# Keeping x in two of five raw weight buffers, and another order of the seven products

## The chip, the core and the metric

The kernel runs on one core of one Trainium2 chip. The metric is the device time of one execution in microseconds (us), the median of the runs shown. The engines are named as in the profile: PE (TensorE) multiplies, PEld is its weight load, DVE (VectorE) and ACT (ScalarE) work element by element, POOL (GpSimd) computes and issues DMAs, SP (SyncE) issues DMAs.

## What is computed

One layer of a streaming encoder over 256 tokens of width 2048, in float32. Cut to what matters here, with `F = 5632`:

```python
def swiglu(h, w_gate, w_up, w_down):
    return (jax.nn.silu(h @ w_gate) * (h @ w_up)) @ w_down

x = x + 0.5 * swiglu(rms_norm(x, ffn1_norm), ffn1_w_gate, ffn1_w_up, ffn1_w_down)
h = rms_norm(x, mix_norm);  proj = h @ w_in            # 2048 -> 4096: u, q, k, v
y_ssm = s5_mixer(u, ...);   y_sb = stick_breaking_attention(q, k, v)
x = x + concat(rms_norm(y_ssm), rms_norm(y_sb)) @ w_out
x = x + 0.5 * swiglu(rms_norm(x, ffn2_norm), ffn2_w_gate, ffn2_w_up, ffn2_w_down)
x = x + rms_norm((p @ w_ple_proj) * sigmoid(rms_norm(x, ple_norm) @ w_ple_gate))
```

## The kernel before

**Split products.** Every weight block comes from DRAM as float32 into a `raw` buffer (128 partitions, four 128-row tiles of 512 columns, 1 MB). A block is split in two halves of two tiles: ACT casts the half to `whi` (L168), DVE takes the rest `wlo = raw - whi` (L171). A half meets both token tiles (`t` = 0, 1) in 12 matmuls of 128x512: hi by hi (L292), hi by lo (L293), lo by hi (L297). There are four `whi` and four `wlo` buffers, so ACT and DVE can be four halves ahead of PE and no more.

**Stages.** `ffn(1)` runs eleven column blocks `f` of gate and up, while `s5_prep` makes the mixer's constants beside it, then four column blocks `n` of down. Then come the mixer, `ffn(2)` of the same shape, and the last gate (`ple`). The transposed hidden rows `hT` are put together by small DMAs from `mid` (L216), into which DVE transposes (L203).

**The seven products.** In `ffn(2)`, for `f` from 1 on, `gemm_seven` treats the first chunk of 512 rows of gate and up together: with the blocks b11, b21 (gate) and b12, b22 (up), seven products P1 to P7 stand for eight. Each is six matmuls (L452, L453, L455). Their weights are either half a raw block (`whi`, `wlo`), or sums of halves: t1 = b11 + b12, t2 = t1 + b22, t4 = t2 + b21, t3 = b12 + b22 (DVE, L459, two `sum` buffers), which are split into `shi` and `slo` (three buffers each). The left sides are the activations or four sums of them that `sum_forms` makes once. The other three chunks of gate and up go the plain way. P1, P2, P4 and P5 gather in `acc` banks, P6, P7, P3 and P8 in two double `aux` banks. At the end of a block DVE adds the `aux` bank into `hh` (L545), multiplies (L547) and transposes (L203).

**Memory.** `raw` has three buffers (8 KB a partition each). x stays in eight tiles of its own, `xt[t][n]` (16 KB a partition in all), from its load (`load_x`, L144) to the end.

**Order.** The code is written in program order, with generators (`put_off`, `step`) that place small work between halves. A scheduler then fixes the order on each engine and gives out the buffers when a program is built; at run time each engine works through its list in order and waits on semaphores.

Of the kernel before, what the change touches and what calls it, by code (L numbers as in the profile page):

```python
# [16 lines left out]
P = 128  # L17
# [9 lines left out]
NB = 512  # L27
# [6 lines left out]
def layer_kernel(ctx: ExitStack, tc: tile.TileContext, a: dict, shapes: dict, out: bass.AP):  # L34
# [18 lines left out]
    xpool = ctx.enter_context(tc.tile_pool(name="xres", bufs=1))  # L53
# [183 lines left out]
    def first_quarters(w, xn):  # L237

        rest = com("h")
        raws = [wp.tile([P, 4, NB], F32, tag="raw", name=uid("raw"), bufs=3) for _ in range(2)]  # L240
# [36 lines left out]

    def weight_halves(w, k0, nk, n0, own=None):

        raw = wp.tile([P, 4, NB], F32, tag="raw", name=uid("raw"), bufs=3)  # L280
        src = w[k0 * P : (k0 + nk) * P, n0 : n0 + NB].rearrange("(j p) n -> p j n", p=P)
        nc.sync.dma_start(raw[:, :nk, :], src)
        return weight_split(raw, nk, own)
# [122 lines left out]
        def rs(self, t):  # L406
            return self.r[:, t : t + 1]

    def sum_forms(parts):

        hi, lo = parts
        whole, sums = com("h"), com("h")
        u = whole.rearrange("p (j t m) -> p j t m", j=4, t=TT)
        nc.vector.tensor_tensor(
            out=whole.rearrange("p (j t) -> p j t", j=4), in0=hi.bitcast(F32), in1=lo.bitcast(F32), op=ALU.add
        )
        s = sums.rearrange("p (z j m) -> p z j m", z=4, j=2)
        up, down = u[:, :2], u[:, 2:]
        for z, (x, y, op) in enumerate((
            (up[:, :, 1], down[:, :, 1], ALU.subtract), (s[:, 0], up[:, :, 0], ALU.subtract),  # L420
            (up[:, :, 0], up[:, :, 1], ALU.subtract), (down[:, :, 0], s[:, 1], ALU.add),
        )):
            nc.vector.tensor_tensor(out=s[:, z], in0=x, in1=y, op=op)
        both = halves("n")
        split(*both, sums.rearrange("p (z t) -> p z t", z=4))
        return both

    def gemm_seven(act, sums, ws, n0, nkt, pool, first, second):

        raws = []  # L430
        for w in ws:
            raw = wp.tile([P, 4, NB], F32, tag="raw", name=uid("raw"), bufs=3)
            nc.sync.dma_start(raw, w[: 4 * P, n0 : n0 + NB].rearrange("(j p) n -> p j n", p=P))
            raws.append(raw)
        b11, b21, b12, b22 = (raw[:, 2 * h : 2 * h + 2, :] for raw in raws for h in range(2))
        parts = act(0)

        def whole(k, t):
            return [[u[:, 2 * k + j, t * P : (t + 1) * P] for j in range(2)] for u in parts]

        def summed(z):
            return [[u[:, z, j * P : (j + 1) * P] for j in range(2)] for u in sums]

        def product(ps, left, src, own, stop):
            hi, lo = (
                (pool if own else wp).tile([P, 2, NB], F32R, tag=s, name=uid(s), bufs=3 if own else None)
                for s in (("shi", "slo") if own else ("whi", "wlo"))
            )
            split(hi, lo, src)
            lh, ll = left  # L450
            for j in range(2):
                nc.tensor.matmul(ps, lhsT=lh[j], rhs=hi[:, j], start=j == 0, stop=False)  # L452
                nc.tensor.matmul(ps, lhsT=ll[j], rhs=hi[:, j], start=False, stop=False)  # L453
            for j in range(2):
                nc.tensor.matmul(ps, lhsT=lh[j], rhs=lo[:, j], start=False, stop=stop and j == 1)  # L455

        def add(x, y):
            t = pool.tile([P, 2, NB], F32, tag="sum", name=uid("sum"), bufs=2)
            nc.vector.tensor_tensor(out=t, in0=x, in1=y, op=ALU.add)  # L459
# [21 lines left out]
        step()  # L481
        put_off(0, first, p1, p67)
        for w, banks, fresh in ((ws[0], [p2, p4], False), (ws[1], [p38[:, :NB], p38[:, NB:]], True)):
            for k0 in range(4, nkt, 4):
                part = act(k0 // 4)
                for half in list(weight_halves(w, k0, 4, n0)):
                    begin = k0 == 4 and half[0] == 0
                    end = k0 + 4 >= nkt and half[0] == 1
                    for t in range(TT):
                        gemm_half({t: banks[t]}, (part, half), (t,), fresh and t == 1 and begin, end)  # L490
                    step()
            if not fresh:
                put_off(0, second, p2, p4, p5)
        return p38

    def ffn(i, xn, nxt, bg=None):
        wg, wu, wd = (a[f"ffn{i}_w_{s}"][0] for s in ("gate", "up", "down"))
# [22 lines left out]
        for f in range(NF):  # L520
# [5 lines left out]
            if sevens and f:  # L526
                sg, hh = com("sg"), com("h")
                gate_cols, up_cols = ([u[:, t * NB : (t + 1) * NB] for t in range(TT)] for u in (sg, hh))

                def opened(p1, p67, g=gate_cols, u=up_cols):  # L530
                    nc.scalar.copy(g[0], p1)
                    nc.vector.tensor_tensor(out=u[0], in0=p67[:, :NB], in1=g[0], op=ALU.add)
                    nc.vector.tensor_tensor(out=u[1], in0=p67[:, NB:], in1=u[0], op=ALU.add)

                def gated(p2, p4, p5, g=gate_cols, u=up_cols, hh=hh):
                    for z, (ps, other) in enumerate(((p2, g[0]), (p4, u[1]))):
# [3 lines left out]
                    nc.vector.tensor_tensor(  # L540
                        out=v, in0=p5.unsqueeze(1).to_broadcast([P, TT, NB]), in1=v, op=ALU.subtract
                    )

                p38 = gemm_seven(xn, sums, (wg, wu), f * NB, KD, sevens, opened, gated)
                nc.vector.tensor_tensor(out=hh, in0=p38, in1=hh, op=ALU.add)  # L545
                for t in range(TT):
                    nc.vector.scalar_tensor_tensor(  # L547
                        out=up_cols[t], in0=up_cols[t], scalar=xn.rs(t), in1=gate_cols[t], op0=ALU.mult, op1=ALU.mult
# [12 lines left out]
            if f == 0 and not bg:  # L561
                both = gemm_pair(xn, ((wg, 0), (wu, 0)), KD)
                pg = next(both)
                sums = sum_forms(xn(0))
            else:
                pg = gemm_block(xn, wg, f * NB, KD, first)
            sg = com("sg")
# [15 lines left out]
                )  # L583
            put_off(2, turned, hp, f, hh)

        def act(k):
            hi, lo = halves("h")
            split(in_32(hi), in_32(lo), hT[k // 2][:, k % 2 * 4 : k % 2 * 4 + 4])
            return hi, lo

        for n in range(ND):
# [743 lines left out]
    for n, side in ((0, 0), (1, 0), (0, 1), (1, 1), (2, 0), (2, 1), (3, 0), (3, 1)):  # L1335
        y, r = ((yss, rss), (ysb, rsb))[side]
        ps = next(both) if n < 2 and not side else gemm_block(lambda k: y[k], sides[side], n * NB, SW // P)
        for t in range(TT):
            nc.vector.scalar_tensor_tensor(
                out=xt[t][n], in0=ps[t], scalar=r[0][:, t : t + 1], in1=xt[t][n], op0=ALU.mult, op1=ALU.add  # L1340
            )
        if side:
            put_off(0 if n == ND - 1 else 2, n2.block, n)
    atp.close()
    mix.close()
# [205 lines left out]
```

## Time and profile before

| | us |
|---|---|
| median of 3 runs | 1872.24 (1870.79 to 1873.25) |
| the profiled execution | 1872.24, its span 1870.4 |
| PE busy | 1859.4 (99%), 9134 matmuls by the page |
| DVE busy | 1310.4 (70%) |
| ACT busy | 996.5 (53%) |
| POOL busy | 50.4 (3%) |
| DMA moved | 400.06 MB, mean 214 GB/s |

The span runs from the first to the last instruction; 1.8 us of the profiled execution's time lie outside it. PE is busy almost all of the span, so a time that falls or rises must show as a gap, or a slower pace, in PE's row of matmuls. The other engines' busy shares say how much room they have to be early.

### The profile page before, as it was taken

The page shows a single profiled execution, that of the slowest core. Times are in us where ns is not written, and L with a number is a line of the kernel's source. Part 1 is how long each engine was busy: PE and PEld are TensorE (multiplying, and loading weights), DVE is VectorE, ACT ScalarE, POOL GpSimd, SP SyncE. Part 2 cuts the span into 40 slices and gives each one's busy share as a digit, 9 for nine tenths or more (in the row PEclk, how much of TensorE's full clock was granted, in tenths as well). Part 3 has the DMA queues.
Part 4 walks back from the last instruction along what each step waited for, and adds up shares of the span by engine and source line. Part 5 has one row for each costly group of instructions (what it writes and reads, how often), then busy time and mean ns, then how long its engine had stood idle before and what let it go on. Part 6 is the DMA issues. An engine that isn't in the chain of part 4 may idle for free.

```text
span 1870.4 us, 23938 instructions
## 1 busy us (share of the span) xinstructions
PE 1859.4 (99%) x9134; PEld 1536.3 (82%) x9134; DVE 1310.4 (70%) x1527; ACT 996.5 (53%) x1151; POOL 50.4 (3%) x84
## 2 busy tenths in 40 slices
PE   9999999999999999999999999999999999999998
PEld 7888888888888888878888888888888888888887
DVE  8867665455576776687567678778787866777655
ACT  7444444444456665456695555445454555666554
POOL 0011000000000000010020000000000000000000
PEclk9999999999999999999999999999999999999999
DMA  8788867766655666675645666575666675656563
GB/s 323 242 278 268 267 208 222 231 217 200 217 196 199 212 199 244 185 248 163 222 147 189 218 205 221 203 220 186 203 205 208 225 228 203 204 202 212 189 224 124
DMA packets 230387, 400.06 MB, mean 214 GB/s; under 512 B 26401, under 2 KB 50337, under 8 KB 229985
## 3 DMA queue, kind: packets, MB, share of 16 engines
q1 hardware_dynamic: 227824, 392.81, 63.7%
q0 software_dynamic: 1728, 4.33, 0.7%
q8 instruction: 71, 1.16, 0.3%
q10 hardware_dynamic: 720, 1.41, 0.2%
q14 instruction: 44, 0.35, 0.1%
HBM read 369.26 MB, written 9.83 MB: 203 GB/s over the span
## 4 chain that ended last, share of the span: by engine, by line
PE 92%; ACT 3%; DVE 2%; DMA 1%; SPq 1%; issue 1%; POOL 0%; DVEq 0%; ACTq 0%; POOLq 0%
PE acc L292 26%; PE acc L297 26%; PE acc L293 26%; PE aux L293 3%; PE aux L292 3%; PE aux L297 3%; ACT whi L168 1%; SPq L1061 1%; PE acc L455 1%; DMA raw<-in_w_in 1%; PE aux L452 1%; PE acc L452 1%; PE acc L453 1%; PE aux L455 1%; PE aux L453 1%
## 5 line engine op out<-in xcount | busy, mean ns | idle before, releaser
L171 DVE TENSOR_TENSOR wlo<-raw,whi 128x1024 fp32r<-128x1024 f32 x656 | 798.2, 1224 | 458.9 <-ACT whi L168 455.3
L168 ACT CAST whi<-raw 128x1024 fp32r<-128x1024 f32 x656 | 686.2, 1053 | 758.7 <-PE acc L293 607.9
L292 PE MATMUL acc<-whi,nhi 128*128 128x512 f32 x1408 | 551.0, 391 | 1.2 <-ACT whi L260 0.5
L293 PE MATMUL acc<-whi,nlo 128*128 128x512 f32 x1408 | 548.2, 389 | 0.0
L297 PE MATMUL acc<-wlo,nhi 128*128 128x512 f32 x1408 | 384.4, 389 | 0.0
L292 PE MATMUL acc<-whi,hhi 128*128 128x512 f32 x816 | 317.6, 389 | 0.0
L293 PE MATMUL acc<-whi,hlo 128*128 128x512 f32 x816 | 317.5, 389 | 0.0
L292 PEld LDWEIGHTS acc<-whi,nhi 128*128 128x128 f32 x1408 | 264.3, 188 | 58.3 <-ACT whi L168 1.7
L297 PEld LDWEIGHTS acc<-wlo,nhi 128*128 128x128 f32 x1408 | 264.2, 188 | 55.6 <-DVE wlo L171 0.4
L293 PEld LDWEIGHTS acc<-whi,nlo 128*128 128x128 f32 x1408 | 264.4, 188 | 54.0
L297 PE MATMUL acc<-wlo,hhi 128*128 128x512 f32 x816 | 221.0, 389 | 0.0
L297 PEld LDWEIGHTS acc<-wlo,hhi 128*128 128x128 f32 x816 | 152.8, 188 | 32.5 <-DVE wlo L171 0.9
L293 PEld LDWEIGHTS acc<-whi,hlo 128*128 128x128 f32 x816 | 153.2, 188 | 32.0
L292 PEld LDWEIGHTS acc<-whi,hhi 128*128 128x128 f32 x816 | 153.1, 188 | 31.8
L171 DVE TENSOR_TENSOR hlo<-hT,hhi 128x1024 fp32r<-128x1024 f32 x88 | 107.1, 1218 | 0.0
L168 ACT CAST hhi<-hT 128x1024 fp32r<-128x1024 f32 x88 | 91.8, 1044 | 0.5 <-PE acc L455 0.4
L292 PE MATMUL aux<-whi,nhi 128*128 128x512 f32 x160 | 62.2, 389 | 0.0
L293 PE MATMUL aux<-whi,nlo 128*128 128x512 f32 x160 | 62.2, 389 | 0.0
L297 PE MATMUL aux<-wlo,nhi 128*128 128x512 f32 x160 | 49.3, 389 | 0.0
L171 DVE TENSOR_TENSOR slo<-sum,shi 128x1024 fp32r<-128x1024 f32 x40 | 48.6, 1214 | 0.4 <-ACT shi L168 0.2
L168 ACT CAST shi<-sum 128x1024 fp32r<-128x1024 f32 x40 | 42.1, 1052 | 11.5 <-DVE sum L459 11.4
L297 PEld LDWEIGHTS aux<-wlo,nhi 128*128 128x128 f32 x160 | 30.0, 188 | 6.2
(312 smaller groups left out, 1314.5 us busy)
## 6 DMA issues: line engine op xcount, KB each, us to landing
raw<-in_ffn_w_up SPq DMA_DIRECT2D x88, 1024.0 KB, 5.9
raw<-in_ffn_w_down SPq DMA_DIRECT2D x88, 1024.0 KB, 5.0
raw<-in_ffn_w_gate SPq DMA_DIRECT2D x86, 1024.0 KB, 5.4
raw<-in_w_in SPq DMA_DIRECT2D x32, 1024.0 KB, 5.5
raw<-in_w_out SPq DMA_DIRECT2D x16, 1024.0 KB, 5.1
raw<-in_w_ple_gate SPq DMA_DIRECT2D x16, 1024.0 KB, 5.1
hT<-mid SPq DMA_DIRECT2D x160, 64.0 KB, 5.0
h<-mid SPq DMA_DIRECT2D x176, 32.0 KB, 3.4
```

Source lines behind the costliest of these rows:

```text
L168: copy = nc.scalar.copy(hi, src)
L171: nc.vector.tensor_tensor(out=lo, in0=src, in1=hi.bitcast(F32), op=ALU.subtract)
L292: nc.tensor.matmul(ps[t], lhsT=lh, rhs=hi[:, j, cols], start=start and j == 0, stop=False)
L293: nc.tensor.matmul(ps[t], lhsT=ll, rhs=hi[:, j, cols], start=False, stop=False)
L297: nc.tensor.matmul(ps[t], lhsT=lh, rhs=lo[:, j, cols], start=False, stop=stop and j == 1)
L452: nc.tensor.matmul(ps, lhsT=lh[j], rhs=hi[:, j], start=j == 0, stop=False)
L453: nc.tensor.matmul(ps, lhsT=ll[j], rhs=hi[:, j], start=False, stop=False)
L455: nc.tensor.matmul(ps, lhsT=lh[j], rhs=lo[:, j], start=False, stop=stop and j == 1)
L1061: nc.sync.dma_start(zt[0][p1 : p1 + HC, z], sv[p0 : p0 + HC, r % 2 * 2 + r // 2])
```

## The change

x loses its own memory. `raw` gets five buffers instead of three, and x is two tiles of the same kind (`place_x`), one per token tile. In `ffn(1)` x is loaded as before, its squares are summed, and its two buffers go back to the weights; after the last gate and up block `fetch_x` takes two buffers again and fetches x by eight POOL DMAs. In the mixer each finished part of x is also written to DRAM (`scr_x`, eight POOL DMAs); after the squares of `ffn2_norm` the two buffers go back to the weights, and before the down products of `ffn(2)` x is fetched from `scr_x`.

The seven products become a class `Seven` with the same arithmetic for one chunk. Their order was P1, P2, P5, P6, P4, P7, P3 and is P1, P5, P6, P4, P7, P2, P3. The sums of activations are made in two `sum` tiles instead of two `h` tiles.

```diff
-    xt = [[xpool.tile([P, NB], F32, name=f"x_{t}_{n}") for n in range(ND)] for t in range(TT)]
+    xt = [[], []]
+    def place_x():
+        for t in range(TT):
+            x = wp.tile([P, ND, NB], F32, tag="raw", name=uid("x"), bufs=5)
+            xt[t][:] = [x[:, n, :] for n in range(ND)]
+    def fetch_x(rows):
+        place_x()
+        for n in range(ND):
+            for t in range(TT):
+                nc.gpsimd.dma_start(xt[t][n], rows[t * P : (t + 1) * P, n * NB : (n + 1) * NB])
+    place_x()
+    scr_x = dramp.tile([T, D], F32, name="scr_x")
...
-        raw = wp.tile([P, 4, NB], F32, tag="raw", name=uid("raw"), bufs=3)
+        raw = wp.tile([P, 4, NB], F32, tag="raw", name=uid("raw"), bufs=5)
...
-        p1, p2 = acc(), acc()
-        product(p1, whole(0, 0), b11, False, True)
-        product(p2, whole(1, 0), b21, False, False)
-        step()
-        t1 = add(b11, b12)
-        p5 = acc()
-        product(p5, summed(0), t1, True, True)
-        t2 = add(t1, b22)
-        p67 = aux()
-        product(p67[:, :NB], summed(1), t2, True, True)
-        step()
-        t4 = add(t2, b21)
-        p4 = acc()
-        product(p4, whole(1, 1), t4, True, False)
-        t3 = add(b12, b22)
-        product(p67[:, NB:], summed(2), t3, True, True)
-        step()
-        p38 = aux()
-        product(p38[:, :NB], summed(3), b22, False, False)
+            self.product(1, whole(0, 0), b11, False, final)
+            t1 = self.add(b11, b12)
+            self.product(5, summed(0), t1, True, final)
+            step()
+            t2 = self.add(t1, b22)
+            self.product(6, summed(1), t2, True, final)
+            t4 = self.add(t2, b21)
+            self.product(4, whole(1, 1), t4, True, final)
+            step()
+            t3 = self.add(b12, b22)
+            self.product(7, summed(2), t3, True, final)
+            self.product(2, whole(1, 0), b21, False, final)
+            step()
+            self.product(3, summed(3), b22, False, final)
...
-                p38 = gemm_seven(xn, sums, (wg, wu), f * NB, KD, sevens, opened, gated)
+                s = Seven(xn, lambda kb: sums[kb], ((wg, f * NB), (wu, f * NB)), sevens)
+                s.chunk(0, shared)
+                put_off(0, opened, s)
+                s.column(0, (1, 2, 3), True)
+                put_off(0, gated, s)
+                s.column(1, (1, 2, 3), True)
...
+        fetch_x(a["x"][0] if bg else scr_x)
...
         if side:
+            for t in range(TT):
+                nc.gpsimd.dma_start(scr_x[t * P : (t + 1) * P, n * NB : (n + 1) * NB], xt[t][n])
```

What the change moves, at two places.

DVE, before, at the start of the seven products of block f = 5 of `ffn(2)`. Here `slo_10415`, `slo_10428`, `slo_10441` and `slo_10453` are the weights of P5, P6, P4 and P7, `wlo_10467` those of P3, and L545, L547 and L203 are the tail of block 4:

```order
L459 TENSOR_TENSOR sum_10424<-sum_10411,raw_10387 128x1024
L171 TENSOR_TENSOR slo_10415<-sum_10411,shi_10414 128x1024
L171 TENSOR_TENSOR wlo_10467<-raw_10387,whi_10466 128x1024
L545 TENSOR_TENSOR h_10060<-aux_10141,h_10060 128x1024
L171 TENSOR_TENSOR slo_10428<-sum_10424,shi_10427 128x1024
L547 SCALAR_TENSOR_TENSOR h_10060<-h_10060,sm_8834,sg_10059 128x512 x2
L459 TENSOR_TENSOR sum_10437<-sum_10424,raw_10385 128x1024
L203 STREAM_TRANSPOSE mid_10462<-h_10060 128x4x4x32
L459 TENSOR_TENSOR sum_10450<-raw_10387 128x1024
L171 TENSOR_TENSOR slo_10441<-sum_10437,shi_10440 128x1024
L203 STREAM_TRANSPOSE mid_10462<-h_10060 128x4x4x32
L171 TENSOR_TENSOR slo_10453<-sum_10450,shi_10452 128x1024
```

Three products' weights (P6, P4, P7) are made after L545, which waits for the last matmul of block 4. DVE after the change, at the same place; `slo_10413`, `slo_10426`, `slo_10439` and `slo_10452` are again P5, P6, P4 and P7, `wlo_10400`, `wlo_10462` and `wlo_10476` are P1, P2 and P3, and L593, L595 are what L545, L547 were:

```order
L184 TENSOR_TENSOR slo_10413<-sum_10410,shi_10412 128x1024
L184 TENSOR_TENSOR wlo_10400<-raw_10395,whi_10399 128x1024
L184 TENSOR_TENSOR slo_10426<-sum_10423,shi_10425 128x1024
L487 TENSOR_TENSOR sum_10436<-sum_10423,raw_10395 128x1024
L184 TENSOR_TENSOR wlo_10462<-raw_10395,whi_10461 128x1024
L487 TENSOR_TENSOR sum_10449<-raw_10397 128x1024
L184 TENSOR_TENSOR slo_10439<-sum_10436,shi_10438 128x1024
L184 TENSOR_TENSOR wlo_10476<-raw_10397,whi_10475 128x1024
L593 TENSOR_TENSOR h_10070<-aux_10155,h_10070 128x1024
L184 TENSOR_TENSOR wlo_10489<-raw_10486,whi_10488 128x1024
L595 SCALAR_TENSOR_TENSOR h_10070<-h_10070,sm_8844,sg_10069 128x512 x2
L184 TENSOR_TENSOR slo_10452<-sum_10449,shi_10451 128x1024
```

All four sums and all products' weights but P7's now stand ahead of the tail of block 4, and P7's stands behind L593, one half of the next column (`wlo_10489`) and L595.

POOL, before, between the mixer's constants (`m`, in `ffn(1)`) and the mixer itself (`dec`):

```order
L860 DMA scr_m_3_105<-m_402_2580 128x1024
L871 MEMSET m_427_2738 128x2048
L945 COPY dec_5821<-rho_117 128x512 x2
L948 MEMSET dec_5821 128x8 x2
L945 COPY dec_6272<-rho_117 128x512 x2
```

POOL after the change, at the same place:

```order
L913 DMA scr_m_3_97<-m_404_2572 128x1024
L924 MEMSET m_429_2730 128x2048
L150 DMA x_3988<-in_x 128x512 x4
L150 DMA x_3989<-in_x 128x512 x4
L998 COPY dec_5823<-rho_109 128x512 x2
L1001 MEMSET dec_5823 128x8 x2
```

The eight fetches of x stand ahead of the first `dec` copy. Eight writes of `scr_x` and eight fetches from it follow in the same way behind the mixer's last POOL work.

More of the change, by code (lines that the diff above doesn't have):

```diff
@@ L239, in first_quarters @@
         rest = com("h")
-        raws = [wp.tile([P, 4, NB], F32, tag="raw", name=uid("raw"), bufs=3) for _ in range(2)]
+        raws = [wp.tile([P, 4, NB], F32, tag="raw", name=uid("raw"), bufs=5) for _ in range(2)]
         src = [w[i * NB : (i + 1) * NB, :NB].rearrange("(j p) n -> p j n", p=P) for i in range(2)]
@@ L424, in sum_forms, with __init__, bank, begin @@
         both = halves("n")
-        split(*both, sums.rearrange("p (z t) -> p z t", z=4))
+        split(*both, sums.rearrange("p j n -> p (j n)").rearrange("p (z t) -> p z t", z=4))
         return both
[L428 to L444, printed above, removed]
+    class Seven:
+        def __init__(self, act, sums, ws, pool):
+            self.act, self.sums, self.ws, self.pool = act, sums, ws, pool
+            self.banks = {}
+            self.begun = set()
+        def bank(self, z):
+            if z not in self.banks:
+                if z in (1, 2, 4, 5):
+                    self.banks[z] = acc()
+                else:
+                    double = aux()
+                    for i, zz in enumerate((6, 7) if z in (6, 7) else (3, 8)):
+                        self.banks[zz] = double[:, i * NB : (i + 1) * NB]
+                    self.banks[6.7 if z in (6, 7) else 3.8] = double
+            return self.banks[z]
+        def begin(self, z):
+            fresh = z not in self.begun
+            self.begun.add(z)
+            return fresh
+        def product(self, z, left, src, own, final):
             hi, lo = (
-                (pool if own else wp).tile([P, 2, NB], F32R, tag=s, name=uid(s), bufs=3 if own else None)
+                (self.pool if own else wp).tile([P, 2, NB], F32R, tag=s, name=uid(s), bufs=3 if own else None)
                 for s in (("shi", "slo") if own else ("whi", "wlo"))
@@ L449, in product @@
             split(hi, lo, src)
+            ps = self.bank(z)
+            begin = self.begin(z)
             lh, ll = left
             for j in range(2):
-                nc.tensor.matmul(ps, lhsT=lh[j], rhs=hi[:, j], start=j == 0, stop=False)
+                nc.tensor.matmul(ps, lhsT=lh[j], rhs=hi[:, j], start=begin and j == 0, stop=False)
                 nc.tensor.matmul(ps, lhsT=ll[j], rhs=hi[:, j], start=False, stop=False)
             for j in range(2):
-                nc.tensor.matmul(ps, lhsT=lh[j], rhs=lo[:, j], start=False, stop=stop and j == 1)
@@ L457, in add @@
-        def add(x, y):
-            t = pool.tile([P, 2, NB], F32, tag="sum", name=uid("sum"), bufs=2)
+                nc.tensor.matmul(ps, lhsT=lh[j], rhs=lo[:, j], start=False, stop=z in final and j == 1)
+        def add(self, x, y):
+            t = self.pool.tile([P, 2, NB], F32, tag="sum", name=uid("sum"), bufs=2)
             nc.vector.tensor_tensor(out=t, in0=x, in1=y, op=ALU.add)
             return t
-        p1, p2 = acc(), acc()
-        product(p1, whole(0, 0), b11, False, True)
-        product(p2, whole(1, 0), b21, False, False)
@@ L481, in gemm_seven, with chunk, whole, summed @@
[L481 to L488, printed above, removed]
+        def chunk(self, kb, final=()):
+            raws = []
+            for w, n0 in self.ws:
+                raw = wp.tile([P, 4, NB], F32, tag="raw", name=uid("raw"), bufs=5)
+                nc.sync.dma_start(
+                    raw, w[4 * kb * P : 4 * (kb + 1) * P, n0 : n0 + NB].rearrange("(j p) n -> p j n", p=P)
+                )
+                raws.append(raw)
+            b11, b21, b12, b22 = (raw[:, 2 * h : 2 * h + 2, :] for raw in raws for h in range(2))
+            parts, sums = self.act(kb), self.sums(kb)
+            def whole(k, t):
+                return [[u[:, 2 * k + j, t * P : (t + 1) * P] for j in range(2)] for u in parts]
+            def summed(z):
+                return [[u[:, z, j * P : (j + 1) * P] for j in range(2)] for u in sums]
+            self.product(1, whole(0, 0), b11, False, final)
[12 more added lines that the diff above has]
+            self.product(3, summed(3), b22, False, final)
+            step()
@@ L489, in gemm_seven, with column @@
+        def column(self, side, kbs, final=False):
+            zs = ((2, 4), (3, 8))[side]
+            w, n0 = self.ws[side]
+            for kb in kbs:
+                part = self.act(kb)
+                for half in list(weight_halves(w, 4 * kb, 4, n0)):
+                    end = final and kb == kbs[-1] and half[0] == 1
                     for t in range(TT):
-                        gemm_half({t: banks[t]}, (part, half), (t,), fresh and t == 1 and begin, end)
+                        ps = self.bank(zs[t])
+                        gemm_half({t: ps}, (part, half), (t,), self.begin(zs[t]), end)
@@ L491, in gemm_seven @@
                     step()
-            if not fresh:
-                put_off(0, second, p2, p4, p5)
-        return p38
+    shared = (1, 5, 6, 7)
     def ffn(i, xn, nxt, bg=None):
@@ L563, in ffn @@
                 pg = next(both)
-                sums = sum_forms(xn(0))
+                sums = [sum_forms(sevens, whole_rows(sevens, xn(0)))]
             else:
@@ L584, in ffn, with rows @@
             put_off(2, turned, hp, f, hh)
+        fetch_x(a["x"][0] if bg else scr_x)
+        def rows(k):
+            return hT[k // 2][:, k % 2 * 4 : k % 2 * 4 + 4]
         def act(k):
             hi, lo = halves("h")
-            split(in_32(hi), in_32(lo), hT[k // 2][:, k % 2 * 4 : k % 2 * 4 + 4])
+            split(in_32(hi), in_32(lo), rows(k))
             return hi, lo
```

36 lines of the change are left out of this document (19 added, 17 removed).

## The prediction

> **What bounds the kernel now.** I read the page first, then the stretches of time, then what PE waits for, then the timelines at one place. The page's first part and its row for the clock:
>
> ```profile
> PE 1859.4 (99%) x9134; PEld 1536.3 (82%) x9134; DVE 1310.4 (70%) x1527; ACT 996.5 (53%) x1151; POOL 50.4 (3%) x84
> PEclk9999999999999999999999999999999999999999
> DMA packets 230387, 400.06 MB, mean 214 GB/s; under 512 B 26401, under 2 KB 50337, under 8 KB 229985
> ```
>
> PE is busy for 1859.4 of 1870.4 us at the full clock, and the change removes no matmul. So it can win only what PE loses to waiting, inside stages that it touches. The stretches of time give that loss: the gate and up stage of `ffn(1)`, and blocks 1 to 10 of `ffn(2)`, where the seven products are. Columns: stretch, its length, then busy time and starts of PE, PEld, DVE, ACT, POOL, the clock, the DMA share, GB/s.
>
> ```profile
> 300.00:700.00 400.00, 400.00 (x1766) 331.20 (x1766) 246.24 (x229) 203.76 (x218) 0.00 (x0) 1.00 0.64 208
> 1096.90:1523.60 426.70, 426.13 (x1866) 348.49 (x1865) 338.58 (x328) 213.71 (x221) 0.00 (x0) 1.00 0.65 212
> ```
>
> In the first, 400.00 / 1766 gives 226.5 ns from matmul to matmul with no gap: a calm pace, and nothing to win in `ffn(1)`. In the second, 1866 x 0.2265 is 422.6 us, and it took 426.7: **4.1 us** are lost in the ten blocks (one matmul miscounted at either edge makes 0.2). PE's own waits hide this, because waits of a few tenths are counted as slow or overlapped matmuls; of the seven products only one wait is listed, and the longest of all lies in the mixer:
>
> ```profile
> PE aux L1190 <- POOL sqg L1206: 1.7, 1, 1.7
> ...
> PE aux L452 <- ACT shi L168: 0.2, 1, 0.2
> ```
>
> Where the 4.1 us lie is read from the first matmul of P1 in blocks 3 to 7, in PE's timeline (start, length):
>
> ```profile
> 1182.26 0.39 PE L452 MATMUL acc<-whi,hhi 128*128 128x512 f32 x1
> 1225.14 0.39 PE L452 MATMUL acc<-whi,hhi 128*128 128x512 f32 x1
> 1267.49 0.39 PE L452 MATMUL acc<-whi,hhi 128*128 128x512 f32 x1
> 1310.42 0.39 PE L452 MATMUL acc<-whi,hhi 128*128 128x512 f32 x1
> 1352.79 0.39 PE L452 MATMUL acc<-whi,hhi 128*128 128x512 f32 x1
> ```
>
> A block has 7 x 6 + 12 x 12 = 186 matmuls, 42.13 us at the calm pace. Blocks 3 and 5 take 42.88 and 42.93, blocks 4 and 6 take 42.35 and 42.37. So odd blocks from 3 on lose about 0.78 us. Four such (3, 5, 7, 9) make 3.1 us, and the other six share the remaining 1.0, about 0.17 each. In block 5 the loss looks like this, on PE, then ACT, then DVE:
>
> ```profile
> 1276.06 0.40 PE L293 MATMUL acc<-whi,hlo 128*128 128x512 f32 x1
> 1276.59 0.50 PE L452 MATMUL aux<-shi,nhi 128*128 128x512 f32 x1
> ...
> 1275.48 1.05 ACT L168 CAST shi<-sum 128x1024 fp32r<-128x1024 f32 x1 [0.75 <-DVE sum L459]
> ...
> 1271.10 1.41 DVE L547 SCALAR_TENSOR_TENSOR h<-h,sm,sg 128x512 f32<-128x512 f32 x2
> 1272.43 1.22 DVE L459 TENSOR_TENSOR sum<-sum,raw 128x1024 f32<-128x1024 f32 x1
> 1273.56 0.71 DVE L203 STREAM_TRANSPOSE mid<-h 128x512 f32<-128x512 f32 x1
> 1274.19 1.19 DVE L459 TENSOR_TENSOR sum<-raw 128x1024 f32<-128x1024 f32 x1
> ```
>
> P7 starts 0.53 us after the matmul before it, 0.30 late. Its cast ended at 1276.53, on a sum that DVE began at 1274.19, behind the tail of block 4 (L547, a transpose). DVE is the engine that is late there, by its order and not by its total.
>
> **The change, part by part.** *Five buffers and the new order.* By the order after the change, all sums and the weights of P1, P5, P6, P4, P2 and P3 stand ahead of the tail of the block before, in odd blocks as in even ones; only P7's stand behind it. What that leaves is a walk from P1's first matmul, with durations from block 4, whose column ended cleanly:
>
> ```profile
> 1225.50 1.22 DVE L545 TENSOR_TENSOR h<-aux,h 128x1024 f32<-128x1024 f32 x1
> 1226.63 1.22 DVE L171 TENSOR_TENSOR slo<-sum,shi 128x1024 fp32r<-128x1024 f32 x1
> 1227.77 1.41 DVE L547 SCALAR_TENSOR_TENSOR h<-h,sm,sg 128x512 f32<-128x512 f32 x2
> 1229.09 1.22 DVE L459 TENSOR_TENSOR sum<-raw 128x1024 f32<-128x1024 f32 x1
> ```
>
> L545 begins 0.36 us after P1 (1225.50 - 1225.14). Start to start, it holds DVE for 1.13, a split for 1.14 and the L547 pair for 1.32. With one split of the next column, L547 and P7's split behind it, P7's `slo` is done at 0.36 + 1.13 + 1.14 + 1.32 + 1.14 = 5.1 us. PE reaches it after 24 matmuls of four products and four with `shi`: 28 x 0.2265 = 6.3 us. **1.2 us to spare.** P7's `shi` reuses P5's buffer, free after P5's last hi matmul, 10 x 0.2265 = 2.3 us; a cast of 1.05 then ends near 3.8 with 0.4 for the hand-over, and is wanted at 24 x 0.2265 = 5.4. So every block should run like the better six now: 10 x 0.17 = 1.7 us lost instead of 4.1. **Gain 2.4 us.** Bounds: 4.1 if the small loss goes too, 0 if a like wait returns at another product; I take 2.4 because blocks 4 and 6 already run PE's products in one piece, as the new order does everywhere.
>
> *x in raw buffers in `ffn(1)`.* The loads of x now wait, on SP, until DVE is done with the first two blocks. SP and ACT at the start:
>
> ```profile
> 15.30 1.93 SPq L144 DMA_DIRECT2D x<-in_x  x4
> ...
> 11.43 1.98 ACT L168 CAST whi<-raw 128x1024 fp32r<-128x1024 f32 x2
> ...
> 30.70 0.63 ACT L394 ACTIVATE sq<-x 128x512 f32<-128x512 f32 x1
> ```
>
> The second block's casts end at 13.4, DVE's split about 1.2 later, at 14.6: before 15.30, when x was issued anyway. Behind it on SP stands a load of up weights. Cost nothing; the cover is the time to the first square at 30.70, and beyond it ACT's queue, with the casts in it, would wait.
>
> *The fetches and writes on POOL.* These rows price them: POOL's issue of a store of 512 KB, the landings of POOL's and SP's transfers, and POOL's next work.
>
> ```profile
> 149.34 0.58 POOL L860 DMA_DIRECT2D scr_m<-m  x1 [1.77 <-DVE m L848]
> 721.80 2.17 POOL L945 COPY dec<-rho 128x512 f32<-128x512 f32 x2 [441.61 <-DVE hlo L171]
> x<-in_x SPq DMA_DIRECT2D x8, 256.0 KB, 8.6
> coef<-scr_coef POOLq DMA_DIRECT2D x32, 64.0 KB, 6.6
> scr_m<-m POOLq DMA_DIRECT2D x4, 512.0 KB, 5.0
> ```
>
> Eight issues of 0.58 and the longest landing, 8.6, make 13.2 us from the first issue. x is wanted at the end of the first down block, 22 halves x 12 matmuls x 0.2265 = 59.8 us after down begins. The POOL work queued behind (`dec`) ran at 721.80; eleven blocks of 16 x 12 matmuls (478 us), 12 us of start and the 59.8 put the end of the first down block near 550. Cost nothing; if the cover went, DVE would hold its splits back. The bytes, 3 x 2.1 MB on 400, are 1.6% at a DMA share of 0.64. One rule speaks against putting this on POOL. The Trainium skill (SBUF — State Buffer, "SBUF: two separate sides") says that descriptors for POOL's DMAs are written through a port shared with DVE, and that DVE can lock it for a whole instruction. By it each issue would wait one DVE instruction more, about 23 us in all, which the 59.8 still cover; the trace has POOL issuing a transfer in 0.58 us in a stage where DVE is busy.
>
> *The return of x's buffers in `ffn(2)`.* The fifth raw load there now waits for the writes of `scr_x`. DVE's last update of x, that load on SP, and how long such a load takes:
>
> ```profile
> 1053.97 1.41 DVE L1339 SCALAR_TENSOR_TENSOR x<-acc,sm,x 128x512 f32<-128x512 f32 x2 [1.09 <-PE acc L297]
> 1064.35 0.53 SPq L282 DMA_DIRECT2D raw<-in_ffn_w_gate  x1
> ...
> raw<-in_ffn_w_gate SPq DMA_DIRECT2D x86, 1024.0 KB, 5.4
> ```
>
> Update done at 1055.4, two issues of 0.58, a landing of 5.0 to 8.6: 1061.6 to 1065.2, so 0 to 0.9 us later than now. Behind it on SP stand four small transfers for the last quarter of the activations. The load serves the ninth half of block 0, which PE reaches eight halves (21.7 us) after about 1054, at 1075.7; landed at 1070.6, cast and split (1.05 + 1.22) at 1072.9 at the latest. Cost nothing, with 2.8 us of cover; beyond that PE waits once.
>
> **The sum.** 1872.24 - 2.4 = **1869.8 us**. The profiled execution took 1872.24, the median of the three runs, so nothing is to be shifted.
>
> **The rivals.** *P7 late in every block* (slower). P7's weights now always stand behind L593, which waits for PE itself. If DVE needs 2.3 us more in that walk (two further instructions), 1.2 are covered and 1.1 are not: ten blocks lose 11 more, 1869.8 + 11 = 1881 us. It outweighs the gain once PE waits more than 0.24 us in a block, at 1.4 us of delay on DVE. For it: the rows of DVE in block 5 and block 4 above follow each other without a gap. Against it: the order puts more work ahead of the tail, and fewer instructions than before stand between the tail and P7. Chance 0.08.
>
> *No gain.* The odd blocks' DVE has the same work as before and pays at another product (P3, or the first half of the next column): 1872.2. For it: DVE is the tightest engine there, 338.58 of 426.70 us. Chance 0.16.
>
> *All of it.* The small losses go as well, because P5 and P6 are ready much earlier: 1872.24 - 4.1 = 1868.1. Against it: P1 to P4 of block 4 were early already, and the block still lost 0.2. Chance 0.14.
>
> **How the numbers follow.** The forecast, a gain of 1.5 to 3.3 us, has 0.62. A difference of 0.2%, 3.7 us, is about what a measurement of this kernel can tell from none, and the three runs differ by 2.5 us. Faster by more needs *all of it* or the best end of the forecast with a lucky run: 0.15. Slower by more is the first rival: 0.08. The rest, 0.77, is within. The range runs from *all of it* less half a microsecond, 1867.6, to *no gain* plus the 1.0 us by which the slowest run of before stood above its median, and as much again for a partly late P7: 1874.2. It leaves out most of the first rival and the lucky end.
>
> **What would show it.** Right: blocks 3, 5, 7 and 9 of `ffn(2)` take 42.3 to 42.4 us like their neighbours, the ten blocks take 424 us instead of 426.7, and DVE's sums L487 stand before L593. Wrong: PE waits for `shi` or `slo` at P7 in every block; a gap at the first `x` update of a down stage, which would mean late fetches; or a pace other than 226.5 ns in stages where nothing waits.

## The result and the profile after

| | before | after |
|---|---|---|
| median, us | 1872.32 (10 runs, 1870.79 to 1873.84) | 1867.64 (10 runs, 1867.14 to 1868.97) |
| the profiled execution, us | 1872.24, span 1870.4 | 1867.14, span 1865.3 |
| blocks 1 to 10 of `ffn(2)`, first P1 to first down matmul, us | 425.78 | 422.80 |
| DMA moved, MB | 400.06 | 406.36 |

The ratio is 0.9975, with a 95% interval of 0.9966 to 0.9985: 4.7 us faster, where 2.4 was forecast. The forecast was 1869.8, in a range from 1867.6 to 1874.2, so the measured time lies at its lower edge. (L452 is now L480, L168 is L181, L171 is L184, L459 is L487, L545 and L547 are L593 and L595, L282 and L433 are L295 and L495.)

The page's row of engines, and the stretches of time after (columns as in the prediction):

```profile
PE 1856.9 (100%) x9134; PEld 1538.6 (82%) x9134; DVE 1309.8 (70%) x1527; ACT 998.9 (54%) x1151; POOL 63.5 (3%) x108
```

```profile
300.00:700.00 400.00, 400.00 (x1767) 331.20 (x1766) 246.25 (x229) 203.84 (x218) 4.40 (x8) 1.00 0.64 208
1095.40:1518.20 422.80, 422.80 (x1861) 349.11 (x1860) 337.43 (x326) 214.51 (x220) 4.36 (x8) 1.00 0.66 213
```

The first stretch is the same as before. In the second, which is the ten blocks, DVE has as much work as before (337 us), yet PE no longer waits. Where P1 starts in blocks 3 to 7, from PE's timeline after:

```profile
1179.96 0.39 PE L480 MATMUL acc<-whi,hhi 128*128 128x512 f32 x1
1222.24 0.39 PE L480 MATMUL acc<-whi,hhi 128*128 128x512 f32 x1
1264.53 0.39 PE L480 MATMUL acc<-whi,hhi 128*128 128x512 f32 x1
1306.80 0.39 PE L480 MATMUL acc<-whi,hhi 128*128 128x512 f32 x1
1349.08 0.39 PE L480 MATMUL acc<-whi,hhi 128*128 128x512 f32 x1
```

All ten blocks take 42.28 us. Before, the four odd ones from 3 on took 42.88 to 42.93, 2.5 us above that together, and the other six another 0.5: 2.98 us in all.

Compared matmul by matmul, the two profiled executions keep a constant distance elsewhere but for three places. At the start after loses 0.11; at 917 before lost 0.46 to a late `whi`; and in the mixer before has this, on PE:

```profile
820.43 1.02 PE L959 MATMUL aux<-ua,m 64*64 64x64 f32 x51
822.90 0.45 PE L959 MATMUL aux<-ua,m 64*64 64x64 f32 x13 [1.45 <-issue]
```

After, the same 64 matmuls run in one piece:

```profile
820.53 1.16 PE L1012 MATMUL aux<-ua,m 64*64 64x64 f32 x64
```

That makes 1.8 of the 5.1 us between the two profiled executions. Whether it belongs to the change was the first open question.

### The profile page after: what moved, and what is told of

It reads as the page before. It is cut to its first block, busy times and chain, and to the rows that moved or that the text cites. A ratio compares the mean times of both kernels' runs of the same rounds, so it can differ in the third digit from the quotient of the medians.

```text
span 1865.3 us, 24011 instructions
## 1 busy us (share of the span) xinstructions
PE 1856.9 (100%) x9134; PEld 1538.6 (82%) x9134; DVE 1309.8 (70%) x1527; ACT 998.9 (54%) x1151; POOL 63.5 (3%) x108
## 2 busy tenths in 40 slices
DMA packets 232306, 406.36 MB, mean 218 GB/s; under 512 B 26784, under 2 KB 50720, under 8 KB 231904
## 3 DMA queue, kind: packets, MB, share of 16 engines
q10 hardware_dynamic: 720, 1.41, 0.2%
## 4 chain that ended last, share of the span: by engine, by line
PE 96%; ACT 2%; DVE 1%; DMA 0%; POOL 0%; issue 0%; SPq 0%; DVEq 0%; POOLq 0%
PE acc L305 27%; PE acc L310 27%; PE acc L306 27%; PE aux L310 3%; PE aux L305 3%; PE aux L306 3%; PE acc L480 1%; PE acc L481 1%; PE acc L483 1%; PE aux L480 1%; PE aux L481 1%; PE aux L483 1%; PE aux L1068 0%; ACT whi L181 0%; DMA raw<-in_ffn_w_gate 0%; ACT nhi L191 0%
## 5 line engine op out<-in xcount | busy, mean ns | idle before, releaser
L184 DVE TENSOR_TENSOR wlo<-raw,whi 128x1024 fp32r<-128x1024 f32 x656 | 797.6, 1224 | 450.4 <-ACT whi L181 443.6
L181 ACT CAST whi<-raw 128x1024 fp32r<-128x1024 f32 x656 | 688.0, 1053 | 765.9 <-PE acc L306 619.7
L184 DVE TENSOR_TENSOR hlo<-hT,hhi 128x1024 fp32r<-128x1024 f32 x88 | 107.2, 1218 | 3.3 <-ACT hhi L181 3.3
L181 ACT CAST hhi<-hT 128x1024 fp32r<-128x1024 f32 x88 | 91.9, 1044 | 2.3 <-DMA hT<-mid 2.3
L181 ACT CAST shi<-sum 128x1024 fp32r<-128x1024 f32 x40 | 42.1, 1054 | 12.5 <-DVE sum L487 9.2
L184 DVE TENSOR_TENSOR slo<-sum,shi 128x1024 fp32r<-128x1024 f32 x40 | 48.6, 1218 | 0.0
L306 PEld LDWEIGHTS aux<-whi,nlo 128*128 128x128 f32 x160 | 30.0, 188 | 6.2
```

Of the source, the lines that this page charges most:

```text
L181: copy = nc.scalar.copy(hi, src)
L184: nc.vector.tensor_tensor(out=lo, in0=src, in1=hi.bitcast(F32), op=ALU.subtract)
L306: nc.tensor.matmul(ps[t], lhsT=ll, rhs=hi[:, j, cols], start=False, stop=False)
```

## Experiments

**Memory alone, and order alone.** The change has two parts. The first kernel keeps the memory and goes back to the old order:

```diff
             self.product(1, whole(0, 0), b11, False, final)
+            self.product(2, whole(1, 0), b21, False, final)
...
             self.product(7, summed(2), t3, True, final)
-            self.product(2, whole(1, 0), b21, False, final)
```

> The change with the seven products back in their old order P1, P2, P5, P6, P4, P7, P3; x still shares the five raw buffers. Theory 'buffers': the gain in ffn(2) comes from two more raw buffers, which let DVE make the sums and splits of the next block ahead of the tail of the block before. DVE's built order already shows that here (P6, P4's weights stand before the tail in odd and even blocks), so the ten blocks should take 422.8 to 423.3 us from the first P1 to the first down matmul (425.78 before, 422.80 after the whole change), every block 42.28 to 42.35. Rival 'order': the order of the products matters most, then odd blocks stay at 42.9 and the ten at 425.5 or more. Total: 1867.6 to 1868.1 by the first, about 1870.5 by the second. The gap of 1.66 us in the middle of 64 small matmuls at 821 us of before: absent if it belongs to before's own program, present or absent at random if it is chance.

The second keeps the new order and goes back to the old memory:

```diff
-            x = wp.tile([P, ND, NB], F32, tag="raw", name=uid("x"), bufs=5)
-            xt[t][:] = [x[:, n, :] for n in range(ND)]
+            xt[t][:] = [xpool.tile([P, NB], F32, name=f"x_{t}_{n}") for n in range(ND)]
...
-        fetch_x(a["x"][0] if bg else scr_x)
...
-        raw = wp.tile([P, 4, NB], F32, tag="raw", name=uid("raw"), bufs=5)
+        raw = wp.tile([P, 4, NB], F32, tag="raw", name=uid("raw"), bufs=3)
```

> The new order of the products alone: three raw buffers, x in memory of its own, no fetch, no scr_x. Theory 'buffers': the odd blocks stay late, since DVE's built order alternates here as before (in block 5 four weights or sums stand behind the tail of block 4, in block 6 only P4's and P7's): ten blocks 425 to 426 us, odd ones 42.7 to 42.9; total within 1 us of before plus or minus the gap at 821. Rival 'order': ten blocks below 423.5, and total below before by 2.5 us or more.

Measured beside 20 runs of before (median 1871.79): memory alone 1867.73 (10 runs), ratio 0.9977 (0.9968 to 0.9986), every block 42.28, the ten 422.80. Order alone **1878.94** (5 runs), ratio 1.0038 (1.0024 to 1.0052), 7 us slower than before: block 1 and the even blocks 42.28, blocks 3, 5 and 7 44.40, block 9 45.98 (more on it under "What stays open"), the ten 432.87. Order alone in block 3, on PE, then ACT, then DVE:

```profile
1185.62 0.74 PE L476 MATMUL aux<-slo,nhi 128*128 128x512 f32 x2
1187.83 0.50 PE L473 MATMUL acc<-shi,hhi 128*128 128x512 f32 x1 [1.47 <-ACT shi L174]
...
1186.73 1.04 ACT L174 CAST shi<-sum 128x1024 fp32r<-128x1024 f32 x1 [1.63 <-DVE sum L480]
...
1183.02 1.41 DVE L588 SCALAR_TENSOR_TENSOR h<-h,sm,sg 128x512 f32<-128x512 f32 x2
1184.35 1.22 DVE L177 TENSOR_TENSOR slo<-sum,shi 128x1024 fp32r<-128x1024 f32 x1
1185.48 1.22 DVE L480 TENSOR_TENSOR sum<-sum,raw 128x1024 f32<-128x1024 f32 x1
```

P4's sum stands behind the tail of the block before (L588), as in before. There P2 came ahead of P5, and six matmuls (1.4 us) that need no sum gave DVE time. With P2 moved towards the end that time is gone. DVE begins P4's sum 5.1 us after P1 here and 4.9 in block 5 of before; but PE came to P4 7.3 us after P1 there, and is free for it 5.8 us after P1 here. It starts P4 1.6 us late, and the block loses 2.1. So theory "buffers" holds, "order" falls, and my own number for order alone was wrong: I had it within 1 us of before. The order is a loss with three buffers and makes no difference with five.

**Four buffers.** Half of x shares:

```diff
+    x0 = xpool.tile([P, ND, NB], F32, name="x_0")
+    xt[0][:] = [x0[:, n, :] for n in range(ND)]
     def place_x():
-        for t in range(TT):
-            x = wp.tile([P, ND, NB], F32, tag="raw", name=uid("x"), bufs=5)
-            xt[t][:] = [x[:, n, :] for n in range(ND)]
+        x = wp.tile([P, ND, NB], F32, tag="raw", name=uid("x"), bufs=4)
+        xt[1][:] = [x[:, n, :] for n in range(ND)]
```

> The change with only one half of x (token tile 1) in a raw buffer: four raw buffers, three while x is held, x of token tile 0 in 8 KB of its own; four DMAs each of fetch and write instead of eight. Theory 'buffers' with the built order of DVE: in odd blocks (3, 5, ...) only P7's sum and weights stand behind the tail of the block before, with L598 pair ahead of the sum; DVE done with P7's sum at 0.36 + 1.13 + 1.14 + 1.32 + 1.2 = 5.2 us after P1, its cast at 6.3, wanted at 5.4: odd blocks lose about 0.7 to 0.9 us, even ones none: ten blocks 425.5 to 427. Rival 'any fourth buffer is enough': ten blocks 422.8 to 423.3, total as after.

1868.84 (11 runs), ratio 0.9983 (0.9975 to 0.9992). Odd blocks from 3 on take 42.45 to 42.47, the others 42.28, the ten 423.53. Both expectations missed. P7's sum does stand behind the tail, but PE's order there has P2 ahead of P7, so only 0.19 us of the wait reaches PE. Block 5 on PE, DVE and ACT:

```profile
1271.62 0.39 PE L486 MATMUL acc<-wlo,hhi 128*128 128x512 f32 x1
1271.89 0.50 PE L483 MATMUL aux<-shi,nhi 128*128 128x512 f32 x1
...
1269.45 1.22 DVE L490 TENSOR_TENSOR sum<-raw 128x1024 f32<-128x1024 f32 x1
...
1270.79 1.05 ACT L184 CAST shi<-sum 128x1024 fp32r<-128x1024 f32 x1 [0.57 <-DVE sum L490]
```

Against 422.80, three buffers (before, in the old order), four and five lose 2.98, 0.73 and 0.0 us: the first extra buffer brings three quarters. In the new order three buffers lose 10.07.

**Before once more.** The kernel before, profiled a second time, unchanged.

> The kernel before, profiled once more, unchanged. If the odd blocks' loss is set by DVE's order it recurs: blocks 3, 5, 7, 9 at 42.85 to 42.95, the rest 42.28 to 42.5. The gap of 1.66 us at 821: if it belongs to the program, it recurs at the same matmul; if it is chance, it is gone or elsewhere, and then 1.66 us of the difference between the two profiled executions is not the change's. The same for the 0.46 us at 917.

1873.42. Blocks 3, 5, 7, 9 again 42.87 to 42.91. The gap at 821 is gone (64 matmuls in 1.40 us), so it was chance, and 1.77 us of the difference between the first two profiles is not the change's. Nor is the 0.46 us at 917: this execution lost 0.30 there, and memory alone the whole 0.46. Instead block 1 took 44.82. On SP, DVE and PE:

```profile
1081.44 0.37 SPq L433 DMA_DIRECT2D raw<-in_ffn_w_up  x1
...
1089.42 1.23 DVE L459 TENSOR_TENSOR sum<-raw,raw 128x1024 f32<-128x1024 f32 x1 [2.63 <-DMA raw<-in_ffn_w_up]
...
1100.57 0.50 PE L452 MATMUL acc<-shi,nhi 128*128 128x512 f32 x1 [1.54 <-DVE h L580]
```

A load that took 8.0 us (median 5.8 in this execution) held DVE's first sum back by 2.63 us, and about 10 us later PE waited for L580, the tail of block 0, which stands behind the sums in DVE's order. That suggested a second gain: in block 5 the loads of the seven products are issued 19.1 and 14.2 us ahead of P1 before, and 25.1 and 24.1 us ahead after.

**Foreign traffic.** To test it, in both kernels:

```diff
+        def burst(u):
+            nc.gpsimd.dma_start(tok[:, :1], u[:, :1])
+            nc.gpsimd.dma_start(sink, tok)
...
+                    burst(u[0])    # in opened
...
+                    burst(g[0])    # in gated
...
+                burst(hh)          # after the block's last product
```

> The kernel before with foreign traffic in blocks 1 to 10 of ffn(2): three times a block POOL copies 512 KB from DRAM to DRAM, after a word that opened, gated and the block's last product give it, so that loads of weights land late at places that the kernel did not choose. Its output is unchanged. Theory 'cover': with three raw buffers a load that lands 2 us late reaches PE, as in the second profile of before (sum waited 2.63 us for a raw, PE lost 1.7); ten blocks take 430 us or more (425.8 without), and the runs rise by 4 us or more over before. Rival 'chance': the late loads were rare and traffic within the DMAs' room (0.65 busy) changes neither kernel by more than 1 us.

> The changed kernel with the same foreign traffic. Theory 'cover': five buffers hold two loads more in hand, about 2 x 5.4 us, so the blocks stay at 42.28 to 42.4 us and the total within 1 us of 1867.6. Rival 'chance': it changes by as much as the kernel before does.

Beside 21 runs of before (1871.68): before with traffic 1874.77 (10 runs), after with traffic 1871.79 (10 runs). That is 3.1 us more for before, and 4.2 more for after than in its own runs (1867.64). In the profiled executions the ten blocks took 429.3 (3.5 more) and 424.83 (2.0 more, all at one place). The traffic's first copy also ran at the start and delayed the first weights, by 2.1 and 3.0 us in these profiles. About 1 us is then left in the medians of either kernel, and the profiled execution of before with traffic (1876.84) was 2.1 us above its median. So neither theory is shown: the totals don't tell the two kernels apart, and the blocks do so in one execution each. What speaks for "cover" is the profile of the changed kernel without traffic: four loads for the sums (L495) took 8.2 to 8.4 us there, and every block still took 42.28. The one place where the changed kernel lost with traffic, in block 7, on DVE and PE:

```profile
1343.24 1.23 DVE L487 TENSOR_TENSOR sum<-raw,raw 128x1024 f32<-128x1024 f32 x1 [2.34 <-DMA raw<-in_ffn_w_up]
...
1355.86 1.22 DVE L603 TENSOR_TENSOR h<-aux,h 128x1024 f32<-128x1024 f32 x1
1356.99 1.22 DVE L184 TENSOR_TENSOR wlo<-raw,whi 128x1024 fp32r<-128x1024 f32 x1
1358.13 1.41 DVE L605 SCALAR_TENSOR_TENSOR h<-h,sm,sg 128x512 f32<-128x512 f32 x2
1359.45 1.22 DVE L184 TENSOR_TENSOR slo<-sum,shi 128x1024 fp32r<-128x1024 f32 x1
...
1360.73 0.74 PE L483 MATMUL aux<-slo,nhi 128*128 128x512 f32 x2 [1.75 <-DVE slo L184]
```

This is the first rival of the prediction, at P7, set off by a late load: DVE's first sum waited 2.34 us for a load of 10.7 us, and DVE worked on without a gap from there. P1 began at 1352.40, so the tail (L603) came 3.46 us after it, P7's split ended at 8.27, and PE wanted it at about 6.4.

**Fewer matmuls.** After the change PE waits nowhere in the ten blocks, so only fewer matmuls can win there, and the question is what DVE allows. The seven products for two chunks instead of one:

```diff
-                s.chunk(0, shared)
+                s.chunk(0)
+                s.chunk(1, shared)
...
-                s.column(0, (1, 2, 3), True)
+                s.column(0, (2, 3), True)
...
-                sums = [sum_forms(sevens, whole_rows(sevens, xn(0)))]
+                sums = [sum_forms(sevens, whole_rows(sevens, xn(k))) for k in range(2)]
```

> The changed kernel with the seven products for the first two chunks of gate and up instead of one, sums and splits on DVE and ACT as before. Theory 'DVE is next': PE's block would fall by 6 matmuls, 42.28 - 1.36 = 40.92 us, but DVE's 33.9 us a block (338.58 / 10) grow by four sums and three splits, 7 x 1.135 = 7.9, to 41.8: blocks of 41.8 to 43.5 us, total 1863 to 1880. Rival 'PE alone': blocks of 40.92, total 1867.6 - 13.6 = 1854.

And with `t1` and `t3` added by `nc.gpsimd.tensor_tensor`:

> As two_chunks, with t1 and t3 of each chunk added on POOL, which is idle in this stage. DVE's block falls by 4 x 1.135 to 37.3 us, under PE's 40.92. POOL's add of 128x1024 is not in the trace; its copies of 128x512 took 1.09 us, so 2.2 to 4.4 us, four of them 9 to 18 us a block. Theory 'DVE is next, and POOL has room': blocks of 40.9 to 41.3, total 1854 to 1858, the fastest of all. Rival 'POOL is late, or slows DVE': blocks of 42.3 or more, total 1868 or more.

Two chunks: 1866.16 (5 runs), ratio 0.9968 (0.9956 to 0.9981). DVE is next, as expected: 98% busy over the first nine blocks, which take 41.21 to 42.54. The tenth takes 42.03, from its P1 at 1474.35 to the first down matmul at 1516.38. The first nine:

```profile
1095.95:1474.30 378.35, 373.91 (x1621) 302.04 (x1620) 371.54 (x359) 217.10 (x226) 0.00 (x0) 1.00 0.64 211
```

With POOL's help it took **1917.58** (4 runs), ratio 1.0242 (1.0228 to 1.0256). The group of DVE's splits of this kernel from 1140 to 1520 us (busy time, mean ns of one), and then DVE's and POOL's timelines at one place:

```profile
L184 DVE TENSOR_TENSOR slo<-sum,shi 128x1024 fp32r<-128x1024 f32 x65 | 108.5, 1675 | 0.3 <-ACT shi L181 0.2
```

```profile
1187.76 1.23 DVE L594 TENSOR_TENSOR h<-aux,h 128x1024 f32<-128x1024 f32 x1
1188.90 2.28 DVE L184 TENSOR_TENSOR slo<-sum,shi 128x1024 fp32r<-128x1024 f32 x1
1191.10 3.56 DVE L596 SCALAR_TENSOR_TENSOR h<-h,sm,sg 128x512 f32<-128x512 f32 x2
...
1186.83 3.27 POOL L487 TENSOR_TENSOR sum<-raw 128x1024 f32<-128x1024 f32 x1 [13.64 <-DVE slo L184]
1191.31 2.80 POOL L487 TENSOR_TENSOR sum<-raw,raw 128x1024 f32<-128x1024 f32 x1 [1.22 <-DVE slo L184]
```

POOL's add takes 2.4 to 3.5 us, and DVE's work beside it is stretched: a split from 1.22 to 2.28 us, the L596 pair from 1.41 to 3.56. L594, which reads one operand from PSUM (`aux`), keeps its 1.23 beside the same add. The Trainium skill (SBUF — State Buffer, "SBUF: two separate sides") says that a DVE operation with two SBUF inputs and a POOL operation that reads SBUF take turns at a shared port, whole instructions at a time, and these rows agree. The split, begun at 1188.90, ended 1.08 us after the add's end at 1190.10, as if it had only run behind it. The theory in my expectation had priced POOL's time alone. The rival "POOL is late, or slows DVE" held, by both its halves: ACT waited 47.8 us in all for POOL's sums, and PE 33.8 us for DVE's `slo` and 8.4 for ACT's `shi`. Part of the 51 us against two chunks is the clock: seven times in the ten blocks the granted clock was 0.5 for 3.41 us, which can make 12 us at most.

**Two chunks in every other block.** Same edit, with `n7 = 2 if f in (2, 4, 6, 8) else 1` chunks; then with block 10 as well.

> As two_chunks (all sums on DVE), but with two chunks of seven products in blocks 2, 4, 6 and 8 of ffn(2) alone. Theory 'DVE is next, and the buffers carry a lead': DVE needs 41.6 us in a block of two chunks against PE's 40.92, and 33.7 against 42.28 in the light block ahead of it, so it is 0.7 us short after a block in which it can get ahead: blocks of two chunks 40.9 to 41.3 us, light ones 42.28, ten blocks 417.4 to 419; total 1867.6 less 3.9 to 5.4, 1862.2 to 1863.7, below both kernels and below two_chunks. Rival 'no lead': five buffers are too few to carry it across a block, blocks of two chunks take 41.9 to 42.5 as in two_chunks and the total stays at 1866 to 1868.

> As two_even, with block 10 too, the last before the down products. Theory 'lead': one more block at 40.9 to 41.3, total 1861 to 1862.6. Rival 'the end of the stage pays': in two_chunks the last block took 45.43 us, its PE waiting before the first down products for DVE; then block 10 takes 42.3 or more and the total is that of two_even or above it.

Beside 8 runs of before (1871.22): 1863.30 (5 runs), ratio 0.9958 (0.9944 to 0.9972), blocks of two chunks 41.05 to 41.10; and 1862.20 (5 runs), ratio **0.9953** (0.9940 to 0.9966), ten blocks 416.74, block 10 41.09. Both "lead" theories held, and both medians lie below those of before and after. The rival for block 10 had no ground: it took the last block of two chunks everywhere at 45.43 us, and that block took 42.03. The ten blocks with block 10 included:

```profile
1096.00:1512.74 416.74, 416.74 (x1832) 343.63 (x1830) 373.19 (x361) 227.32 (x235) 4.36 (x8) 1.00 0.66 216
```

DVE has about as much work (373 us) as in the nine blocks above, but spread over ten so that PE never waits.

## Why the prediction was right, and where it was off

**The total: inside the range, partly by luck.** 1867.64 lies 0.04 us above the lower bound of 1867.6, and the gain is almost twice the 2.4 that was forecast. The blocks account for 2.98; the sum had no term for the other 1.7. The rival "all of it" (1868.1) came nearest in time, but of the 4.1 us it counted on only 2.98 were there to be won.

**What bounds it: right.** What the runs show the change to have won is PE's waits in `ffn(2)`; `ffn(1)` won nothing.

**The ten blocks: mechanism right, the small loss wrong.** The odd blocks' loss was forecast to go, and went: 2.5 us, where 2.4 was forecast as the whole gain. "So every block should run like the better six now: 10 x 0.17" was the wrong term. Against 42.13 us a block at the calm pace, 42.28 remains everywhere after, also in blocks without a wait, so about 0.15 belongs to the block itself; what could go of the other six blocks' loss was 0.5 us, and it went. The stage's gain was 2.98. My reason for the forecast, that the new order runs the products in one piece, was no reason: the order alone cost 7 us, and the memory alone gave it all. Of "Five buffers and the new order", the buffers were the cause. The walk of DVE rested on the built order, which came from five buffers.

**The walk to P7: half the spare time.** Block 5 after, on DVE:

```profile
1265.56 1.22 DVE L593 TENSOR_TENSOR h<-aux,h 128x1024 f32<-128x1024 f32 x1
1266.69 1.21 DVE L184 TENSOR_TENSOR wlo<-raw,whi 128x1024 fp32r<-128x1024 f32 x1
1267.83 1.41 DVE L595 SCALAR_TENSOR_TENSOR h<-h,sm,sg 128x512 f32<-128x512 f32 x2
1269.15 1.22 DVE L184 TENSOR_TENSOR slo<-sum,shi 128x1024 fp32r<-128x1024 f32 x1
```

P1 began at 1264.53. The steps are those forecast, but L593 came 1.03 us after P1, not 0.36, since DVE was still at a split. P7's `slo` was done at 5.84 us and used at 6.41: 0.57 us to spare, not 1.2. The rival stayed off by half a microsecond, and appeared when traffic made DVE late.

**The fetches, the writes, the return of x's buffers: free, as forecast, the last by another way.** POOL's fetches and last writes, a split on DVE beside the last fetches, the first update of x in each down stage, and the fifth raw load on SP with what stands ahead of it, after:

```profile
459.81 0.56 POOL L150 DMA_DIRECT2D x<-in_x  x1 [179.52 <-DMA hT<-mid]
468.64 0.55 POOL L150 DMA_DIRECT2D x<-in_x  x1 [1.51 <-issue]
1053.02 1.20 POOL L1397 DMA_DIRECT2D scr_x<-x  x2 [20.55 <-DVE x L1392]
1488.96 1.16 POOL L150 DMA_DIRECT2D x<-scr_x  x2 [434.74 <-DMA hT<-mid]
1493.51 3.25 POOL L150 DMA_DIRECT2D x<-scr_x  x6 [3.39 <-DVE wlo L184]
...
1494.56 1.22 DVE L184 TENSOR_TENSOR wlo<-raw,whi 128x1024 fp32r<-128x1024 f32 x1 [1.45 <-ACT whi L181]
...
550.36 1.29 DVE L647 SCALAR_TENSOR_TENSOR x<-acc,x 128x512 f32<-128x512 f32 x2 [1.09 <-PE acc L310]
1578.02 1.29 DVE L647 SCALAR_TENSOR_TENSOR x<-acc,x 128x512 f32<-128x512 f32 x2 [1.08 <-PE acc L310]
...
1054.51 7.91 SPq L229 DMA_DIRECT2D h<-mid  x12
1062.65 0.40 SPq L295 DMA_DIRECT2D raw<-in_ffn_w_gate  x1
```

Both updates waited for PE alone. The fetches began about 30 us before the down products, as soon as buffers fell free, so 82 us lay between the last issue and the first update, where I had counted 59.8 from the first issue. Eight issues took 9.4 and 7.8 us, not 4.6: POOL waited 3.2 and 3.4 us in between for a buffer that DVE still read. An issue itself took 0.55 us. The Trainium skill (SBUF — State Buffer, "SBUF: two separate sides") says that POOL can't write descriptors while DVE runs an operation in a two-port mode. That each issue would wait for a DVE instruction, as the prediction took it, doesn't show in these rows: six fetches in a row were issued in 3.25 us, across a DVE split. (The 1.51 us ahead of the last fetch in `ffn(1)` have no releaser in the profile.)

The raw load came within its forecast of 1061.6 to 1065.2, but that was luck. The forecast had it wait for the writes, with 5.0 to 8.6 us for a landing. The last write landed at 1056.15, 2.5 us after its issue, and SP issued the load only behind twelve small transfers of the activations, the last of them at 1061.82.

**What stays open.** The medians differ by 4.7 us for the change and by 4.1 for memory alone, each beside its own runs of before (medians in four sets: 1871.2 to 1872.3); the blocks differ by 2.98. Of the rest between the profiles, the gap at 821 and the 0.46 us at 917 are not the change's. Both profiles of before hold one stall of 1.7 to 2.5 us. Those of after, memory alone and four buffers hold none like it outside the start and the wait at L1243 that all have (L1190 before), and their runs spread over 0.9 to 1.8 us against 2.7 to 5.0 of before. The fastest runs on record, 1870.36 of 59 of before and 1867.14 of ten after, differ by 3.2 us, close to the blocks' 2.98. That more buffers make chance stalls rarer fits this, but the traffic runs did not show it, so 1.1 to 1.7 us stay unexplained.

Block 9 of order alone (45.98 us where 44.40 was usual) looks like one more such stall and is none. PE waits there as in block 3, and then eight matmuls take 0.43 us each instead of 0.23. The stretch, with the granted clock third from the end:

```profile
1448.40:1451.81 3.41, 3.41 (x9) 2.66 (x9) 3.41 (x5) 1.05 (x1) 0.00 (x0) 0.50 0.98 345
```

The granted clock was 0.5 for 3.41 us. Why there and not in blocks 3, 5 and 7, with the same wait, the runs don't show.

## What to carry to other kernels

Buffers decide more than whether a transfer is on time: where a scheduler fixes each engine's order, they decide how far ahead an engine's work may be put, and so what stands behind the tail of the step before. A reordering that looks harmless can be worth nothing with enough buffers and cost much without, so try each part of a change alone. Once PE has no gap left, put extra work on the next engine unevenly, a heavy block behind a light one, so that the lead made in one is spent in the other.

## What the runs showed of the hardware

POOL arithmetic beside DVE is not free: while POOL added two 128x1024 operands (2.4 to 3.5 us each), DVE's splits of the sums took 1.68 us in the mean, and its splits of the weights 1.34, instead of 1.22. Eight DMA issues by POOL in the same stage held no DVE work up that PE noticed. The clock can drop for a few microseconds in the middle of a busy kernel on one core: in the profiles it was 0.5 for 3.41 us once with the order alone and seven times with POOL's adds, and PE's list of waits shows nothing of it. And one profiled execution can hold a chance stall of 1.7 us (64 small matmuls broken by 1.45 us of "issue"), more than a third of the 4.7 us that were to be explained; a second profile of the unchanged kernel told it apart.
